# First-norm modulation on TensorE for both samples, and a first FFN block fed tile by tile

## The chip, the core and the metric

One core of one Trainium2 chip runs the kernel. A core has TensorE (PE: matmul; PEld is its weight load), VectorE (DVE), ScalarE (ACT), GpSimd (POOL) and SyncE (SP), which here issues every DMA. The metric is the device time of one execution in microseconds, the median of several runs. All data is fp32; large products are made from rounded parts ("high" and "low"), three matmuls for each pair of tiles.

## What is computed

One layer of a diffusion backbone, for 1024 latent tokens and 256 context tokens of width 1024. Cut to what matters here:

```python
m = silu(cvec) @ w_mod + b_mod                # nine vectors of 1024, for c (latent) and for c_ctx (context)
def pre(h, g_pre, shift, scale):
    return rms_norm(h, g_pre) * (1.0 + scale) + shift
ffn1 = lambda h, m: 0.5 * post(swiglu(pre(h, norm_pre[0], m[0], m[1]), w_gate, w_up, w_down), norm_post[0], m[2])
x, h_c = x + ffn1(x, mx), h_c + ffn1(h_c, mc)   # mx from c, mc from c_ctx
# then the token mixers (attention and a gated recurrence), and a second FFN for x alone
```

Vector 0 (shift) and vector 1 (scale) of either sample have to be known before the first FFN can read its input.

## The kernel before

Activations lie transposed: width on the 128 partitions in KT = 8 slices, tokens along the free axis, in three chunks `CH`: 0 and 1 of 512 latent tokens (sample 0), 2 of 256 context tokens (sample 1). The first FFN walks the 2816 hidden columns in 11 blocks of two 128-column tiles `f`. Block 0 runs `block_by_chunk`: for a chunk `gu` makes the gate and up products (4 PSUM tiles named bank; with `k_outer` the contraction index k runs outermost, so that k = 0 can start when one input slice is there), then `down` multiplies with two rows of the down weights into PSUM tiles y. Later blocks run `block`, over all chunks. `heads` says which chunks share one pass of block 0: chunks 0 and 1 first, then chunk 2 in a pass of its own, which loads the block's weights again.

`load_w` loads 512 KB to a staging tile st (three buffers), casts the high part on ScalarE (line 91) and subtracts on VectorE or GpSimd for the low part (line 92). In block 0 GpSimd does that for three of the four gate and up tiles.

`start1(i)` prepares chunk i: `row_norms` (squares, column sums on TensorE at line 217, the reciprocal root by `rsqrt` in eleven small VectorE steps, a diagonal, and at line 233 a matmul with ones that spreads it over the partitions; cb is the PSUM of both), then `build_u` with four operations for each slice: GpSimd multiplies by the row, ScalarE applies scale and shift (line 459) and casts `uh` (line 460), GpSimd subtracts for `ul` (line 461). Before each slice, `mod_first` loads two 512 KB tiles of w_mod (one output per partition) and VectorE makes a dot product of each with the conditioning row `crow[s]` (line 153); it does so for sample 0 before chunk 0 and again for sample 1 while chunk 1 is built. The other seven vectors come later as tasks (`mod_stream`) spread over the middle blocks.

Each engine runs its instructions in a fixed order that a scheduler made when the kernel was built; `tc.high_priority()` moves some forward. DMAs are issued in SP's order, and one that waits for its buffer holds all behind it.

Of the kernel before, what the change touches and what calls it, by code (L numbers as in the profile page):

```python
# [14 lines left out]
ALU = mybir.AluOpType  # L15
# [32 lines left out]
def f32(ap):  # L48
    return ap.bitcast(F32)
# [3 lines left out]
def hybrid_block(ctx: ExitStack, tc: tile.TileContext, xT, cc, cols, w_mod, w_gate, w_up, w_down, w_tok, w_col,  # L53
# [101 lines left out]
    def mod_first(d, s, st, split=False):  # L155
        for m in (1, 0):
            t = st()
            sp.dma_start(out=t, in_=w_mod[m * KT + d])
            to = mods[:, m, d, s:s + 1]
            if split and m == 0:  # L160
                pool.tensor_tensor(t, t, crow[s], op=ALU.mult)
                act.activation(t, t, AF.Copy, accum_out=to)
            else:
                dot(t, t, crow[s], to)
            finish_mod(m, slice(d, d + 1), slice(s, s + 1))

    def mod_stream(ms, junkp):
        halves = []

        def step(m, d):  # L170
            ss = range(2 if m < 5 else 1)
            st = stp.tile([P, D], F32, name="st")
            sp.dma_start(out=st, in_=w_mod[m * KT + d])
# [12 lines left out]
        return [(lambda m=m, d=d: step(m, d)) for m in ms for d in range(KT)]  # L186
# [118 lines left out]
    def ffn(which, chunks, heads, ends, ys, wp, hp, psA, psB, finish, start, pump, tasks=(), before=lambda sub: None):  # L305
# [10 lines left out]
        def gu(ws, sub, k_outer=False, pump=None):  # L316
# [7 lines left out]
            for j, e, k in order:  # L324
                w = ws[j][e]
# [97 lines left out]
    with f1_ctx:  # L423
# [27 lines left out]
        def build_u(i, before):  # L451
            o, n = CH[i]
            s = 1 if i == 2 else 0
            for d in range(KT):
                before(d)
                u32 = nrm.tile("xt", n) if i in (2,) else sl(n)
                h = uh[i][:, d, :]
# [5 lines left out]
        spare = ys[2].rearrange("p a b -> p (a b)").rearrange("p (t d) -> p t d", d=D)  # L463
        turn = [0]

        def stage():
            return stp.tile([P, D], F32, name="st")

        def next_spare():
            turn[0] += 1  # L470
            return spare[:, turn[0] % 2] if turn[0] % 3 else stage()

        def start1(i):
            if i == 0:
                with tc.high_priority():
                    row_norms(0)

                def before(d):
                    mod_first(d, 0, next_spare)
                    if d == 4:  # L480
                        fetch(1)
                    if d == 7:
                        row_norms(1)

                build_u(0, before)
                fetch(2)
                sp.dma_start(out=crow[1], in_=cc[1:2].partition_broadcast(P))
                act.activation(crow[1], crow[1], AF.Silu)
            elif i == 1:
                def before(d):  # L490
                    if d == 4:
                        row_norms(2)
                    mod_first(d, 1, stage)

                build_u(1, before)
            else:
                build_u(2, lambda d: None)

        sp.dma_start(out=crow[0], in_=cc[0:1].partition_broadcast(P))
        sp.dma_start(out=col, in_=cols)  # L500
        act.activation(crow[0], crow[0], AF.Silu)
        fetch(0)
        def finish1(sub):
# [3 lines left out]
        ffn(0, FULL, ((1, FULL[0:2]), (1, FULL[2:3])),  # L507
            ((((2, 0, 256), (0, 0, 512)),) * 2, (((1, 0, 512),), ((1, 0, 256), (1, 256, 256)))),
            ys, w1, hp, psA, psB, finish1, start1, nrm.pump, tasks)
# [658 lines left out]
def layout(a):  # L1168
# [5 lines left out]
    def cols(w, n=P):  # L1174
# [6 lines left out]
        "cc": np.concatenate([a["c"], a["c_ctx"][None]]),  # L1181
        "cols": lines(a["b_mod"], a["norm_pre"], a["norm_post"], a["hg_norm"], a["hg_lower_bound"]),
        "w_mod": a["w_mod"][0].T.reshape(9 * KT, P, D),
# [31 lines left out]
```

## Time and profile before

| | us |
|---|---|
| median of 3 runs | 2861.35 (2856.90 to 2863.21) |
| the profiled execution | 2862.51 |
| its span, first to last instruction | 2860.7 |
| TensorE busy | 2730.9 (95%) |
| VectorE busy | 1542.4 (54%) |
| ScalarE busy | 1009.6 (35%) |
| GpSimd busy | 352.8 (12%) |

TensorE's share is near the whole span, so what an edit is worth depends on where TensorE waits. Busy TensorE is not TensorE at its peak: a matmul can be held by its weight load or run at the lower of two granted clock levels (0.50 or 1.00 in the column PEclk; before the first recorded change, at 40.9 us, the column reads 1.00 whatever the level was). In the order lists and in the trace one fp32 matmul of the norm stands as two records.

### The profile page before, as it was taken

Reading aid. Unit: us, or ns where it says so; the run is one execution under the profiler, and the core shown is the slowest. Engines: PE = TensorE matmul, PEld = TensorE weight load, DVE = VectorE, ACT = ScalarE, POOL = GpSimd, SP = SyncE. Lnnn points to the kernel's source line nnn. Section 1 sums busy time; section 2 is a strip of 40 time slices with the busy share of each in tenths; the row PEclk is TensorE's granted clock in tenths of the full one; section 3 lists DMA queues with packets and bytes.
Section 4 is the critical chain, followed back from the end, with each engine's and each line's share of the span. In section 5 each row is a group of like instructions: output and inputs, shape, how many; then the busy total and the mean of one; then the engine's idle time right before and its main releaser. Section 6 shows DMA issues by size and latency. Waiting matters only on the chain.

```text
span 2860.7 us, 37319 instructions
## 1 busy us (share of the span) xinstructions
PE 2730.9 (95%) x15032; PEld 2332.9 (82%) x15032; DVE 1542.4 (54%) x2893; ACT 1009.6 (35%) x1495; POOL 352.8 (12%) x276
## 2 busy tenths in 40 slices
PE   4799999999999988999999988899989999999998
PEld 3588888888888888889988877787878888888887
DVE  7756554444435785656655488644474333333336
ACT  3521111111112442566776565343354211111123
POOL 4600000000000332100000132212141000000002
PEclk9899999999999999999999999999999999999999
DMA  6552222322212432211111233254353211111123
GB/s 228 175 161 93 77 75 81 96 85 85 67 45 64 136 108 71 74 50 50 38 57 44 79 136 124 78 183 141 111 170 107 74 52 52 45 45 46 58 67 103
DMA packets 114702, 259.48 MB, mean 91 GB/s; under 512 B 12256, under 2 KB 51808, under 8 KB 114528
## 3 DMA queue, kind: packets, MB, share of 16 engines
q1 hardware_dynamic: 114528, 257.08, 28.4%
q8 instruction: 118, 1.93, 0.3%
q14 instruction: 56, 0.46, 0.0%
HBM read 216.67 MB, written 40.37 MB: 90 GB/s over the span
## 4 chain that ended last, share of the span: by engine, by line
PE 71%; DVE 10%; issue 8%; ACT 4%; DMA 4%; POOL 2%; SPq 0%; DVEq 0%; POOLq 0%; ACTq 0%
PE bank L101 12%; PE bank L102 12%; PE bank L100 12%; PE y L100 6%; PE y L101 6%; PE y L102 6%; PE fb L101 2%; PE fb L102 2%; PE fb L100 2%; PE S L749 2%; PE bank L765 1%; DMA gt<-gate_d 1%; PE po L778 1%; DVE w L92 1%; PE po L779 1%
## 5 line engine op out<-in xcount | busy, mean ns | idle before, releaser
L100 PE MATMUL bank<-uh,w 128*128 128x512 f32 (+1 forms) x1952 | 715.2, 368 | 15.0 <-ACT uh L460 12.5
L101 PE MATMUL bank<-ul,w 128*128 128x512 f32 (+1 forms) x1952 | 717.7, 368 | 7.0 <-POOL ul L461 6.9
L102 PE MATMUL bank<-uh,w 128*128 128x512 f32 (+1 forms) x1952 | 716.2, 367 | 1.8 <-DVE w L92 1.8
L91 ACT CAST w<-st 128x1024 fp32r<-128x1024 f32 x234 | 243.3, 1049 | 785.9 <-PE y L101 439.8
L100 PEld LDWEIGHTS bank<-uh,w 128*128 128x128 f32 x1952 | 370.8, 190 | 75.5 <-ACT uh L460 14.4
L101 PEld LDWEIGHTS bank<-ul,w 128*128 128x128 f32 x1952 | 371.5, 190 | 68.8 <-POOL ul L461 10.1
L102 PEld LDWEIGHTS bank<-uh,w 128*128 128x128 f32 x1952 | 372.1, 191 | 60.7 <-DVE w L92 2.7
L92 DVE TENSOR_TENSOR w<-st,w 128x1024 fp32r<-128x1024 f32 x212 | 267.2, 1268 | 255.1 <-ACT w L91 253.1
L355 DVE TENSOR_TENSOR y<-y,y 128x512 f32<-128x512 f32 (+1 forms) x416 | 255.0, 619 | 202.7 <-PE y L102 200.8
L100 PE MATMUL y<-h,w 128*128 128x512 f32 (+1 forms) x736 | 283.4, 387 | 8.9 <-ACT h L341 3.9
L102 PE MATMUL y<-h,w 128*128 128x512 f32 (+1 forms) x736 | 281.1, 383 | 1.4 <-DVE w L92 1.4
L101 PE MATMUL y<-h,w 128*128 128x512 f32 (+1 forms) x736 | 281.7, 383 | 0.3 <-DVE h L342 0.3
L340 DVE TENSOR_TENSOR sl<-bank,sl 128x512 f32<-128x512 f32 (+1 forms) x114 | 70.5, 620 | 373.4 <-PE bank L102 365.7
L268 POOL TENSOR_TENSOR y<-y,xt 128x512 f32<-128x512 f32 x48 | 64.0, 1352 | 1551.7 <-DVE y L267 891.4
L100 PE MATMUL fb<-uh,w 128*128 128x512 f32 (+1 forms) x576 | 222.6, 387 | 0.0
L102 PE MATMUL fb<-uh,w 128*128 128x512 f32 (+1 forms) x576 | 220.1, 382 | 0.0
L101 PE MATMUL fb<-ul,w 128*128 128x512 f32 (+1 forms) x576 | 220.0, 382 | 0.0
L100 PEld LDWEIGHTS y<-h,w 128*128 128x128 f32 x736 | 138.4, 189 | 42.2 <-ACT h L341 5.7
L102 PEld LDWEIGHTS y<-h,w 128*128 128x128 f32 x736 | 139.0, 189 | 28.9 <-DVE w L92 2.0
L101 PEld LDWEIGHTS y<-h,w 128*128 128x128 f32 x736 | 139.1, 189 | 25.4 <-DVE h L342 0.8
L341 ACT CAST h<-sl 128x512 fp32r<-128x512 f32 (+1 forms) x92 | 55.3, 602 | 281.0 <-DVE sl L340 280.7
L339 ACT ACTIVATE sl<-bank 128x512 f32<-128x512 f32 (+1 forms) x114 | 61.0, 537 | 189.5 <-PE bank L102 189.5
(225 smaller groups left out, 4307.2 us busy)
## 6 DMA issues: line engine op xcount, KB each, us to landing
st<-in_w_mod SPq DMA_DIRECT2D x77, 512.0 KB, 3.7
st<-in_w_gate SPq DMA_DIRECT2D x56, 512.0 KB, 3.7
st<-in_w_up SPq DMA_DIRECT2D x56, 512.0 KB, 3.7
st<-in_w_down SPq DMA_DIRECT2D x56, 512.0 KB, 3.6
st<-in_w_col SPq DMA_DIRECT2D x32, 512.0 KB, 3.7
gate_d<-ft SPq DMA_DIRECT2D x32, 256.0 KB, 2.4
gt<-gate_d SPq DMA_DIRECT2D x32, 256.0 KB, 2.8
st<-in_w_o SPq DMA_DIRECT2D x16, 512.0 KB, 3.7
```

Of the source, the lines that this page charges most:

```text
L91: act.copy(hi, st)
L92: eng.tensor_tensor(lo, st, f32(hi), op=ALU.subtract)
L100: pe.matmul(ps, lh, rh, start=first, stop=False)
L101: pe.matmul(ps, lh, rl, start=False, stop=False)
L102: pe.matmul(ps, ll, rh, start=False, stop=last)
L268: pool.tensor_tensor(yj, yj, xt, op=ALU.add)
L339: act.activation(sl, pg, AF.Silu)
L340: dve.tensor_tensor(sl, pu, sl, op=ALU.mult)
L341: act.copy(hh, sl)
L355: dve.tensor_tensor(yd, py, yd, op=ALU.add)
L749: pe.matmul(S[:, cs_], qT[:, (s * 2 + t) * P:(s * 2 + t + 1) * P], kT[g][:, cs_], start=(s == 0), stop=(s == 1))
L765: pe.transpose(pt[:, (a * 2 + t) * P:(a * 2 + t + 1) * P], prob[t][:, kt * P:(kt + 1) * P], ident)
```

## The change

- Vectors 0 and 1 are made by TensorE for both samples at once: a 512 KB tile of w_mod01 now has the contraction on its partitions; eight matmuls of 128x128 weights against two columns (`cs_t`, both conditioning vectors) give a [128, 2] result (line 164 of the changed kernel), and one small VectorE operation finishes it. There are 16 such tiles, where sample 0 and sample 1 had 16 loads each. Four spare buffers take turns.
- Slices are fed inside the product: `feed(i, k)` is called at each k of chunk 0's first product, makes the vectors two slices ahead and builds the slice one ahead.
- `build_u` has three operations: VectorE multiplies by scale and row, ScalarE adds the shift and casts `uh`, VectorE makes `ul`. GpSimd has no part in block 0 any more; all four weight subtractions are VectorE's.
- The loads of chunks 1 and 2 follow all vector tiles; `row_norms(1)` and `row_norms(2)` move behind the products of the chunk ahead.
- `heads` is one pass of block 0 over all three chunks; four gate and up tiles and two down rows are loaded once less.

```diff
-    def mod_first(d, s, st, split=False):
+    def mod_first(d, st, bank):
         for m in (1, 0):
             t = st()
-            sp.dma_start(out=t, in_=w_mod[m * KT + d])
-            to = mods[:, m, d, s:s + 1]
...
-                dot(t, t, crow[s], to)
-            finish_mod(m, slice(d, d + 1), slice(s, s + 1))
+            sp.dma_start(out=t, in_=w_mod01[m * KT + d])
+            ps = bank()[:, 0:2]
+            for k in range(KT):
+                pe.matmul(ps, t[:, k * P:(k + 1) * P], cs_t[:, k, :], start=(k == 0), stop=(k == KT - 1))
+            if m == 1:
+                dve.tensor_scalar(gpre[:, 0, d, :], ps, bias1[:, d:d + 1], npre[:, 0, d:d + 1],
+                                  op0=ALU.add, op1=ALU.mult)
+            else:
+                dve.tensor_scalar(mods[:, 0, d, :], ps, bias_c[:, 0, d:d + 1], None, op0=ALU.add)
...
             for j, e, k in order:
+                if k_outer and j == 0 and e == 0:
+                    feed(i, k)
...
-            eng = pool if b == 0 and which == 0 else dve
-            gw = [(gcol(w_gate, f, eng), gcol(w_up, f, eng if f == fs[0] else dve)) for f in fs]
+            gw = [(gcol(w_gate, f), gcol(w_up, f)) for f in fs]
...
-                pool.tensor_tensor(u32, ys[i][:, d, :], rows[i], op=ALU.mult)
-                act.activation(u32, u32, AF.Identity, bias=mods[:, 0, d, s:s + 1], scale=gpre[:, 0, d, s:s + 1])
-                act.copy(h, u32)
-                pool.tensor_tensor(ul[i][:, d, :], u32, f32(h), op=ALU.subtract)
+            dve.scalar_tensor_tensor(u32, ys[i][:, d, :], gpre[:, 0, d, s:s + 1], rows[i], op0=ALU.mult, op1=ALU.mult)
+            act.activation(h, u32, AF.Identity, bias=shift)
+            dve.scalar_tensor_tensor(ul[i][:, d, :], u32, shift, f32(h), op0=ALU.add, op1=ALU.subtract)
...
+        def feed1(i, k):
+            if i:
+                return
+            if k == 0:
+                build_u(0, 0)
+            if k + 2 < KT:
+                mod_first(k + 2, next_spare, nrm.bank)
+            elif k == KT - 2:
+                fetch(1)
+                fetch(2)
+                for s in range(2):
+                    sp.dma_start(out=crow[s], in_=cc[s:s + 1].partition_broadcast(P))
+            if k + 1 < KT:
+                build_u(0, k + 1)
...
-        ffn(0, FULL, ((1, FULL[0:2]), (1, FULL[2:3])),
+        ffn(0, FULL, ((1, FULL),),
```

What TensorE has in a row at its start, before:

```order
L217 MATMUL cb<-ones,acc 128x1 x4
L233 MATMUL cb<-sq,ones 128x128 x4
L100 MATMUL bank<-uh_90,w 128x512
L101 MATMUL bank<-ul_93,w 128x512
L102 MATMUL bank<-uh_90,w 128x512
```

And after (lines 221 and 237 are the 217 and 233 of before):

```order
L221 MATMUL cb<-ones,acc 128x1 x4
L237 MATMUL cb<-sq,ones 128x128 x4
L164 MATMUL cb<-cs_t,crow_135 128x2 x8
L164 MATMUL cb<-cs_t,y_125 128x2 x8
L164 MATMUL cb<-cs_t,crow_136 128x2 x8
L100 MATMUL bank<-uh_90,w 128x512 x3
L164 MATMUL cb<-cs_t,y_125 128x2 x8
L100 MATMUL bank<-uh_90,w 128x512
L101 MATMUL bank<-ul_93,w 128x512
L102 MATMUL bank<-uh_90,w 128x512
```

Three vector tiles now stand ahead of chunk 0's first product; the others follow one by one, with six or seven of its 96 matmuls between two of them, and 16 behind the last.

TensorE where chunk 0's products end and chunk 1's begin (uh_90 is chunk 0's input, uh_91 chunk 1's), before:

```order
L100 MATMUL y<-h,w 128x512
L101 MATMUL y<-h,w 128x512
L100 MATMUL y<-h,w 128x512
L101 MATMUL y<-h,w 128x512
L102 MATMUL y<-h,w 128x512 x2
L100 MATMUL bank<-uh_91,w 128x512 x3
```

And after:

```order
L102 MATMUL bank<-uh_90,w 128x512
L221 MATMUL cb<-ones,acc 128x1 x4
L237 MATMUL cb<-sq,ones 128x128 x4
L100 MATMUL y<-h,w 128x512
L101 MATMUL y<-h,w 128x512
L100 MATMUL y<-h,w 128x512
L101 MATMUL y<-h,w 128x512
L100 MATMUL bank<-uh_91,w 128x512 x2
L102 MATMUL y<-h,w 128x512 x2
```

The two steps of chunk 1's norm, which stood inside chunk 0's products, now stand between the two chunks.

ScalarE around the same place, after (line 450 squares chunk 1 or 2, 346 and 348 are the gated unit of chunk 0, 455 copies the spread row):

```order
L464 ACTIVATE uh_90<-sl,mods 128x512 x8
L450 ACTIVATE acc<-y_117 128x512
L450 ACTIVATE sq<-y_117 128x512
L346 ACTIVATE sl<-bank 128x512
L450 ACTIVATE sq<-y_117 128x512
L346 ACTIVATE sl<-bank 128x512
L348 CAST h<-sl 128x512
L450 ACTIVATE sq<-y_117 128x512 x2
L348 CAST h<-sl 128x512
L450 ACTIVATE sq<-y_117 128x512 x3
```

Before, the eight squares of chunk 1 stood among the casts of chunk 0's slices; now six of them come after the first gated unit.

## Rows read from the trace of the kernel before

**Rows 1.** The page's busy time of each engine.

```profile
PE 2730.9 (95%) x15032; PEld 2332.9 (82%) x15032; DVE 1542.4 (54%) x2893; ACT 1009.6 (35%) x1495; POOL 352.8 (12%) x276
```

**Rows 2.** Busy us (instructions) by engine, granted clock, DMA; stretches of 40 us.

```profile
core 0: us, PE busy (x) PEld busy (x) DVE busy (x) ACT busy (x) POOL busy (x), PEclk, DMA share, GB/s
0.00:40.00 40.00, 9.80 (x28) 7.32 (x28) 26.32 (x49) 15.79 (x21) 15.78 (x14) 1.00 0.66 227
40.00:80.00 40.00, 29.04 (x101) 21.48 (x102) 32.07 (x61) 16.85 (x29) 19.56 (x13) 0.83 0.68 234
...
200.00:240.00 40.00, 40.00 (x210) 34.19 (x209) 20.88 (x45) 5.12 (x8) 0.00 (x0) 1.00 0.25 79
```

**Rows 3.** TensorE timeline: start us, us, line, out<-in, count [idle before <-releaser].

```profile
170.20 0.28 PE L102 MATMUL y<-hc,w 128*128 128x256 f32 x1
```

**Rows 4.** TensorE timeline: the records of chunk 0's norm.

```profile
14.64 1.87 PE L217 MATMUL cb<-ones,acc 128*128 128x1 f32 x8 [14.64 <-DVE acc L446]
23.40 2.08 PE L233 MATMUL cb<-sq,ones 128*128 128x128 f32 x8 [6.89 <-DVE sq L227]
```

**Rows 5.** TensorE timeline, chunk 0: wide matmuls and their spacing.

```profile
44.36 0.79 PE L101 MATMUL bank<-ul,w 128*128 128x512 f32 x1 [2.90 <-POOL ul L461]
...
46.66 0.63 PE L102 MATMUL bank<-uh,w 128*128 128x512 f32 x1
47.09 0.63 PE L100 MATMUL bank<-uh,w 128*128 128x512 f32 x1
...
47.87 0.40 PE L102 MATMUL bank<-uh,w 128*128 128x512 f32 x1
...
77.12 0.39 PE L101 MATMUL bank<-ul,w 128*128 128x512 f32 x1
77.35 0.39 PE L102 MATMUL bank<-uh,w 128*128 128x512 f32 x1
```

**Rows 6.** TensorE timeline at 952 us: column sums among wide matmuls.

```profile
952.31 0.95 PE L217 MATMUL cb<-ones,acc 128*128 128x1 f32 x8
953.11 0.48 PE L100 MATMUL bank<-uh,w 128*128 128x512 f32 x1
```

**Rows 7.** Busy us by engine and granted clock, as rows 2, four short stretches.

```profile
157.10:160.30 3.20, 1.77 (x14) 1.55 (x13) 1.82 (x4) 2.77 (x5) 0.00 (x0) 1.00 0.00 0
160.50:163.70 3.20, 2.75 (x16) 2.27 (x16) 3.20 (x5) 1.23 (x2) 0.00 (x0) 1.00 0.78 200
928.50:931.70 3.20, 2.23 (x14) 2.01 (x15) 3.10 (x8) 0.80 (x2) 0.00 (x0) 1.00 0.98 267
931.90:935.10 3.20, 3.20 (x9) 2.52 (x8) 1.19 (x3) 0.00 (x0) 0.00 (x0) 0.50 1.03 408
```

**Rows 8.** TensorE timeline within the third of those stretches.

```profile
930.04 0.95 PE L217 MATMUL cb<-ones,acc 128*128 128x1 f32 x8
```

**Rows 9.** VectorE timeline, chunk 0's norm and weights.

```profile
9.92 4.67 DVE L446 TENSOR_TENSOR acc<-acc,sq 128x512 f32<-128x512 f32 x6
...
17.10 2.25 DVE L196 SCALAR_TENSOR_TENSOR nw<-rc 128x4 f32<-128x4 f32 x1
...
21.88 0.16 DVE L196 SCALAR_TENSOR_TENSOR nw<-rc 128x4 f32<-128x4 f32 x1
...
27.08 1.44 DVE L92 TENSOR_TENSOR w<-st,w 128x1024 fp32r<-128x1024 f32 x1 [1.61 <-ACT w L91]
```

**Rows 10.** ScalarE timeline: copy of a spread row, cast of a weight.

```profile
25.51 0.58 ACT L449 COPY acc<-cb 128x512 f32<-128x512 f32 x1 [8.69 <-PE cb L233]
...
78.67 1.05 ACT L91 CAST w<-st 128x1024 fp32r<-128x1024 f32 x1 [0.40 <-DMA st<-in_w_down]
```

**Rows 11.** TensorE timeline: the spreads of chunks 1 and 2.

```profile
73.05 1.05 PE L233 MATMUL cb<-sq,ones 128*128 128x128 f32 x8
...
106.91 1.19 PE L233 MATMUL cb<-sq,ones 128*128 128x128 f32 x4 [8.71 <-DVE sq L227]
```

**Rows 12.** The page's DMA issues: queue, count, KB each, median us to landing.

```profile
st<-in_w_mod SPq DMA_DIRECT2D x77, 512.0 KB, 3.7
```

More of the change, by code (lines that the diff above doesn't have):

```diff
@@ L52, in hybrid_block @@
 @with_exitstack
-def hybrid_block(ctx: ExitStack, tc: tile.TileContext, xT, cc, cols, w_mod, w_gate, w_up, w_down, w_tok, w_col,
+def hybrid_block(ctx: ExitStack, tc: tile.TileContext, xT, cc, cT, cols, w_mod01, w_mod, w_gate, w_up, w_down, w_tok, w_col,
                  w_mrg, w_o, q_norm, k_norm, cos_t, sin_t, mask_f, mask_b, out_t, out_e):
@@ L153, in dot @@
         dve.scalar_tensor_tensor(junk, st, 1.0, row, op0=ALU.mult, op1=ALU.mult, accum_out=out)
[L155 removed]
+    cs_t = const.tile([P, KT, 2], F32, name="cs_t")
+    bias1 = const.tile([P, KT], F32, name="bias1")
+    def mod_first(d, st, bank):
         for m in (1, 0):
             t = st()
[L158 to L165 removed]
+            sp.dma_start(out=t, in_=w_mod01[m * KT + d])
[5 more added lines that the diff above has]
+                                  op0=ALU.add, op1=ALU.mult)
+            else:
+                dve.tensor_scalar(mods[:, 0, d, :], ps, bias_c[:, 0, d:d + 1], None, op0=ALU.add)
     def mod_stream(ms, junkp):
@@ L172, in step @@
             st = stp.tile([P, D], F32, name="st")
-            sp.dma_start(out=st, in_=w_mod[m * KT + d])
+            sp.dma_start(out=st, in_=w_mod[(m - 2) * KT + d])
             if d == 0:
@@ L303, in drain, with ffn @@
                 self.pump()
-    def ffn(which, chunks, heads, ends, ys, wp, hp, psA, psB, finish, start, pump, tasks=(), before=lambda sub: None):
+    def ffn(which, chunks, heads, ends, ys, wp, hp, psA, psB, finish, start, pump, tasks=(), before=lambda sub: None,
+            feed=lambda i, k: None):
         tasks = list(tasks)
@@ L449, in row_norms, with build_u @@
             act.copy(rows[i], ps)
-        def build_u(i, before):
-            o, n = CH[i]
+        def build_u(i, d):
+            n = CH[i][1]
             s = 1 if i == 2 else 0
[L454 to L457, printed above, removed]
-                pool.tensor_tensor(u32, ys[i][:, d, :], rows[i], op=ALU.mult)
-                act.activation(u32, u32, AF.Identity, bias=mods[:, 0, d, s:s + 1], scale=gpre[:, 0, d, s:s + 1])
-                act.copy(h, u32)
-                pool.tensor_tensor(ul[i][:, d, :], u32, f32(h), op=ALU.subtract)
+            u32 = nrm.tile("xt", n) if i == 2 else sl(n)
+            h = uh[i][:, d, :]
+            shift = mods[:, 0, d, s:s + 1]
+            dve.scalar_tensor_tensor(u32, ys[i][:, d, :], gpre[:, 0, d, s:s + 1], rows[i], op0=ALU.mult, op1=ALU.mult)
+            act.activation(h, u32, AF.Identity, bias=shift)
+            dve.scalar_tensor_tensor(ul[i][:, d, :], u32, shift, f32(h), op0=ALU.add, op1=ALU.subtract)
         spare = ys[2].rearrange("p a b -> p (a b)").rearrange("p (t d) -> p t d", d=D)
+        spares = [spare[:, 0], crow[0], spare[:, 1], crow[1]]
         turn = [0]
-        def stage():
-            return stp.tile([P, D], F32, name="st")
         def next_spare():
             turn[0] += 1
-            return spare[:, turn[0] % 2] if turn[0] % 3 else stage()
+            return spares[turn[0] % 4]
         def start1(i):
@@ L476, in start1 @@
                     row_norms(0)
[L478 to L485, printed above, removed]
-                fetch(2)
[L487 to L495, printed above, removed]
-            else:
-                build_u(2, lambda d: None)
-        sp.dma_start(out=crow[0], in_=cc[0:1].partition_broadcast(P))
+                for d in range(2):
+                    mod_first(d, next_spare, nrm.bank)
+            elif i == 1:
+                row_norms(1)
+                for d in range(KT):
+                    build_u(1, d)
+            else:
+                row_norms(2)
+                for d in range(KT):
+                    build_u(2, d)
+        def feed1(i, k):
[7 more added lines that the diff above has]
+                fetch(1)
+                fetch(2)
+                for s in range(2):
+                    sp.dma_start(out=crow[s], in_=cc[s:s + 1].partition_broadcast(P))
+            if k + 1 < KT:
+                build_u(0, k + 1)
+            else:
+                for s in range(2):
+                    act.activation(crow[s], crow[s], AF.Silu)
+        sp.dma_start(out=cs_t, in_=cT)
         sp.dma_start(out=col, in_=cols)
-        act.activation(crow[0], crow[0], AF.Silu)
+        act.activation(cs_t, cs_t, AF.Silu)
+        dve.tensor_scalar(bias1, bias_c[:, 1], 1.0, None, op0=ALU.add)
         fetch(0)
@@ L1181, in layout @@
         "cc": np.concatenate([a["c"], a["c_ctx"][None]]),
+        "cT": np.concatenate([a["c"], a["c_ctx"][None]]).reshape(2, KT, P).transpose(2, 1, 0),
         "cols": lines(a["b_mod"], a["norm_pre"], a["norm_post"], a["hg_norm"], a["hg_lower_bound"]),
-        "w_mod": a["w_mod"][0].T.reshape(9 * KT, P, D),
+        "w_mod01": cols(a["w_mod"][0][:, 0:2 * D]).reshape(2 * KT, P, D),
+        "w_mod": a["w_mod"][0][:, 2 * D:].T.reshape(7 * KT, P, D),
         "w_gate": np.stack([cols(w).reshape(NF, P, D) for w in a["ffn_w_gate"][0]]),
```

2 lines of the change are left out of this document (1 added, 1 removed).

## The prediction, made before the changed kernel was run

> **What bounds the kernel now.** I read the page first: TensorE is busy 2730.9 us, 95% of the 2860.7 us span [rows 1]. So the kernel as a whole is a TensorE kernel, and a saving on VectorE, ScalarE or the DMA queue counts only where TensorE waits for it. The table of 40 us stretches says where that is [rows 2]: TensorE is busy 9.8 of the first 40 us, 29 of the next, and all of the forty from 200 us on. The change touches only what happens before that point, so I read that part as a timeline of each engine and asked one thing: when is block 0 of the first FFN done? Its last matmul ends at 170.5 us; 13 matmuls of block 1 (3 us) already stand ahead of it, so block 0 costs 167.5 us [rows 3]. Two marks cut this in stages:
>
> - Start to 25.5 us: squares of chunk 0, the column sums (eight one-column records, 14.64), the reciprocal root on VectorE, the spread (23.40) [rows 4].
> - 25.5 to 77.7 us: the 96 wide (512-column) matmuls of chunk 0. Back to back they would need 22 us at the upper clock level, where they stand some 0.2275 us apart (0.23 by 77.12 and 77.35), and 41 us at the lower, 0.427 apart (46.66, 47.09) [rows 5]. The rest is waiting for the input tiles, which wait for the dot products of VectorE.
> - 77.7 to 167.5 us: everything else of block 0, 89.8 us.
>
> **The change part by part.** *Added on TensorE: the 16 vector tiles.* Each is eight fp32 matmuls of two columns with weights of their own, so 16 records, as the column sums give two records for each matmul. The trace has no two-column ones; the nearest rows are the one-column and the 128-column ones, and they cost the same: at the lower level eight take 1.87 us and 2.08 us with the tail of the last, some 0.21 us each [rows 4]; at the upper level eight of one column push the next wide matmul from 952.31 to 953.11, 0.10 us each [rows 6]. So a tile costs 16 x 0.21 = 3.4 us or 16 x 0.10 = 1.6 us, and the sixteen 54 or 26 us. None of it lies beside other work of TensorE: it runs in order, and the new order puts three tiles ahead of the first wide matmul and one after each six or seven of them. A gain below zero is excluded, since no TensorE work is taken away in exchange.
>
> *Which level?* In the trace the stretch from 928.5 to 931.7 has TensorE busy 2.23 us, 0.95 of them column sums (930.04), and the granted clock is 0.50 right behind it; from 157.1 to 160.3 it is busy less, 1.77 us, but all of it 512- and 256-column work, and the clock stays at 1.00 [rows 7, 8]. The small matmuls did not hold the upper level. It also rises late: at 47.8 only after eight wide matmuls had stood without a gap from 44.36 on [rows 5]. In the changed order at most seven stand between two vector tiles. So I take the lower level (1.2 GHz) from the start of the stage until the last tile; behind it 16 wide ones stand together. The upper level is the other bound.
>
> The Trainium skill (TensorE: Matmul & The Clock Gate, Why this matters for your kernels) advises to keep TensorE continuously busy to get the full clock. Read literally, this dense stream of tiny matmuls would be at 2.4 GHz; no run here shows it, and it is the first rival below.
>
> *The start* does not move. VectorE takes over three weight subtractions from GpSimd (1.44 us each, 27.08), set between the steps of the root, some 4 us; but there one step of 128x4 (17.10) had taken 2.25 us and the next as much beside GpSimd's subtractions, against 0.16 for the same step at 21.88 [rows 9]. That 4 us goes. I keep 25.5.
>
> *End of chunk 0's products*, at the lower level: 25.5 + 54 + 96 x 0.427 (41) = 120.5, less 1 us for the last 16, in which the level may rise: 119.5 us, against 77.7. The build of the input hides: per step of the contraction VectorE has two 512-element operations (0.8 us each by six in 4.67) and ScalarE one (0.58) [rows 9, 10], against 12 us of TensorE. The loads hide too: 512 KB land in 3.7 us [rows 12], and a vector tile's buffer is taken again after four tiles, over 20 us of TensorE.
>
> *Moved: the norm of chunk 1.* Today its spread (73.05) and the column sums before it stand inside the products of chunk 0 [rows 11]. In the changed program both stand between the products of chunk 0 and those of chunk 1, and ScalarE has the sigmoid-weighted units of chunk 0 mixed with the last six squares. Behind the end of the products: two more steps of the gated unit and five or six squares of 0.6 us, some 4.6 us (0.58 for 512 elements, 25.51) [rows 10]; from the last addition (14.59) to the spread row's copy (26.1) chunk 0's chain took 11.5 us [rows 9, 10], 4.2 of them beside GpSimd's subtractions, so 7.3; then one weight cast (1.05, 78.67) and a start of 0.3. TensorE waits 13.3 us. On SP the loads of chunk 1, chunk 2, the two conditioning rows and the first down weights now queue behind the vector tiles, and chunk 2's last half waits for the last tile's matmuls, 6.5 us before the products end; the 3 MB in front of and with the down weights take 13 us at 234 GB/s [rows 2], which lands 8 us behind the end and is covered by those 13.3.
>
> *Chunk 1's products:* 100 matmuls x 0.2275 = 22.8, and 2.5 for restarting at the lower level. *Norm of chunk 2,* after them in the new order: 6.5 us (the same chain, two columns fewer, squares done). *Chunk 2's products,* half as wide: 96 x 0.12 = 11.5, and 2.5 again. *Down products:* 90 x 0.2275 + 48 x 0.12 = 26.2, with 4.5 for the second down weight, whose buffers only come free now, and for evacuation. Sum: 13.3 + 25.3 + 6.5 + 14 + 30.7 = 89.8 us, the same as today's 89.8.
>
> *Removed:* the sixteen loads and dots for sample 1, GpSimd's whole part, and the second loading of four block-0 weights and two down weights. They held TensorE up in the third stage (8.7 us before 106.91 for chunk 2's spread alone [rows 11]); those savings are already in the 89.8, and the norm waits take their place. From block 1 on both programs do the same work.
>
> **Sum.** 119.5 + 89.8 = 209.3 us against 167.5: 41.8 us later. The profiled execution took 2862.5 us for a span of 2860.7, 1 us above the median of 2861.35, so the sum goes on the median: 2903 us. Its bounds: a norm wait of 10 to 17 us and tiles of 3.2 to 3.6 us give 2896 to 2910.
>
> **Rivals.** *1. The tiny matmuls keep the clock up.* All tiles but the first two at the upper level: 25.5 + 26 + 22 + 4 = 77.5 us, then the same 89.8: 167.3 against 167.5, no change, 2861; with the bounds of the norm wait 2857 to 2867. For it: the stage would be dense. Against it: [rows 7, 8].
>
> *2. The level rises and falls within the stage.* Seven wide matmuls in a row nearly repeat what preceded the rise at 47.8. If a third to two thirds of the 95 us run at the upper level, 16 to 32 us come back: 2871 to 2887; edges 2867 to 2895.
>
> *3. Faster: the weight loads hide.* The decider is whether the tiles' 256 weight loads run beside the wide matmuls. Then only the first three tiles cost their 3.4 us; with the wide ones at the upper level the stage ends at 25.5 + 10 + 22 + 4 = 61.5, 16 us earlier: 2845. It decides from less than 1.6 us per tile on. Against it: in the steady part loads for wide matmuls already hold the weight port 34.2 of 40 us [rows 2], and column sums placed among wide matmuls pushed them by the full 0.10 each [rows 6].
>
> By a rule of the Trainium skill (TensorE: Matmul & The Clock Gate, Part 2, step by step) weight loads are pulled ahead of running matmuls; that is this rival's mechanism, and [rows 6] show it hiding nothing where small matmuls follow each other.
>
> **How the numbers follow.** Lower level throughout: 0.50. Rival 2: 0.23. Rival 1: 0.17. Rival 3: 0.10. About 0.2% (5.7 us) is what a measurement of this kernel can tell from no change. Slower by more: 0.50 + 0.23 + 0.03 of rival 1's upper edge = 0.76; same 0.14; faster 0.10. The range runs from 2863, inside rival 1, to 2912, 2 us above the first case's own bound: it leaves out rival 3, half of rival 1 and little above, 2 in 10.
>
> **What would show it.** Right: the vector tiles' 16 records take about 3.4 us each, wide matmuls between them 0.43 apart, granted clock 0.5 until near 115 us, chunk 0's last product near 119 us, then a TensorE gap of some 13 us before chunk 1, block 0 done near 209 us, and the same pace after. Wrong: records of 0.10 us and 0.23 us spacing before 60 us (rival 1), alternating levels (rival 2), tiles that do not delay the wide matmuls (rival 3); or a gap before chunk 1 far from 13 us, which would fault my reading of the moved norm.

## The result, and the profile after

| | before | after |
|---|---|---|
| median | 2860.8 us | 2903.7 us (4 runs, 2894.04 to 2905.37) |
| ratio | | 1.014, 95% interval 1.0126 to 1.0154 |
| profiled execution | 2862.51 us | 2904.91 us |

The change makes the kernel 1.4% slower. The predicted 2903 us is met by luck: in the traces below block 0 is done 26 us earlier than forecast, and the rest of the kernel takes 26 us longer.

The page's busy time of each engine, after (before: [rows 1]):

```profile
PE 2793.9 (96%) x15288; PEld 2379.1 (82%) x15288; DVE 1496.5 (52%) x2846; ACT 991.4 (34%) x1466; POOL 269.3 (9%) x222
```

TensorE has 256 records more (the vector tiles) and 63 us more busy time; VectorE and GpSimd have less to do. The first two stretches of [rows 2], after:

```profile
0.00:40.00 40.00, 21.97 (x93) 20.92 (x93) 16.16 (x37) 12.47 (x17) 0.70 (x6) 1.00 0.62 212
40.00:80.00 40.00, 40.00 (x197) 36.16 (x198) 8.45 (x18) 2.90 (x4) 0.00 (x0) 1.00 0.38 114
```

TensorE no longer waits from 40 to 80 us (40.0 busy, before 29.0): the starved stage became a dense one. What the dense stage consists of stands in the TensorE timeline, after (start us, us, line, out<-in, count [idle before <-releaser]):

```profile
12.42 1.87 PE L221 MATMUL cb<-ones,acc 128*128 128x1 f32 x8 [12.42 <-DVE acc L452]
19.90 2.08 PE L237 MATMUL cb<-sq,ones 128*128 128x128 f32 x8 [5.61 <-DVE sq L231]
21.77 3.41 PE L164 MATMUL cb<-cs_t,crow 128*128 128x2 f32 x16
25.04 3.55 PE L164 MATMUL cb<-cs_t,y 128*128 128x2 f32 x16
28.45 3.55 PE L164 MATMUL cb<-cs_t,crow 128*128 128x2 f32 x16
...
43.96 0.63 PE L100 MATMUL bank<-uh,w 128*128 128x512 f32 x1
44.39 0.63 PE L101 MATMUL bank<-ul,w 128*128 128x512 f32 x1
...
64.44 2.06 PE L164 MATMUL cb<-cs_t,crow 128*128 128x2 f32 x16
...
67.84 1.84 PE L164 MATMUL cb<-cs_t,y 128*128 128x2 f32 x16
69.54 0.49 PE L100 MATMUL bank<-uh,w 128*128 128x512 f32 x1
...
93.30 0.39 PE L102 MATMUL bank<-uh,w 128*128 128x512 f32 x1
99.84 1.86 PE L221 MATMUL cb<-ones,acc 128*128 128x1 f32 x8 [6.15 <-DVE acc L452]
104.25 2.08 PE L237 MATMUL cb<-sq,ones 128*128 128x128 f32 x8 [2.55 <-DVE sq L231]
108.25 0.80 PE L100 MATMUL y<-h,w 128*128 128x512 f32 x1 [1.93 <-ACT w L91]
...
133.56 0.50 PE L221 MATMUL cb<-ones,acc 128*128 128x1 f32 x4
...
140.92 1.01 PE L100 MATMUL bank<-uh,w 128*128 128x256 f32 x3 [1.52 <-ACT uh L464]
...
183.56 0.28 PE L102 MATMUL y<-hc,w 128*128 128x256 f32 x1
```

Read from the top: three vector tiles follow each other without a gap for 10 us at 3.4 us each, with wide matmuls 0.43 apart behind them (43.96, 44.39): the lower level, 1.2 GHz, although TensorE was dense. The trace records the rise to 2.4 GHz at 64.9 us, inside the tile at 64.44; from there a tile costs 1.7 us (67.84 to the next wide matmul at 69.54). Chunk 0's products end at 93.7 us, then come 14.5 us with only the norm of chunk 1, and block 0's last matmul ends at 183.8; two matmuls of block 1 stand ahead of it, so block 0 is done at 183.4 us, 15.9 later than before. The other 26 us come later. I matched the TensorE records of the two traces by tile, counted from the end, and took the difference of their starts:

| us of the kernel before | lag of after |
|---|---|
| 200 to 900 (rest of the first FFN) | 15.8, falling to 15.2 |
| 1110 | 20.3 |
| 1900 | 18.1 |
| 2010, start of the second FFN | 20.2 |
| 2160 | 24.2 |
| 2800 | 42.0 |

In the second FFN nothing was changed. From 2150 us (before) and 2170 us (after) to its end both profiles have it at the upper level and with less than 1 us of TensorE waits; yet it does less in the same time. One stretch of 100 us, before and after (columns as in [rows 2]):

```profile
2300.00:2400.00 100.00, 100.00 (x443) 82.71 (x442) 37.23 (x48) 15.59 (x20) 0.00 (x0) 1.00 0.14 43
```

```profile
2300.00:2400.00 100.00, 100.00 (x430) 80.48 (x429) 34.45 (x45) 15.25 (x20) 0.00 (x0) 1.00 0.16 48
```

443 matmuls are 226 ns each, 430 are 233: wide matmuls start 226 to 227 ns apart before and 230 to 238 after, with the same engines at work beside them.

### The profile page after: what moved, and what is told of

It reads as the page before. It is cut to its first block, busy times and chain, and to the rows that moved or that the text cites. A ratio compares the mean times of both kernels' runs of the same rounds, so it can differ in the third digit from the quotient of the medians.

```text
span 2902.8 us, 37652 instructions
## 1 busy us (share of the span) xinstructions
PE 2793.9 (96%) x15288; PEld 2379.1 (82%) x15288; DVE 1496.5 (52%) x2846; ACT 991.4 (34%) x1466; POOL 269.3 (9%) x222
## 5 line engine op out<-in xcount | busy, mean ns | idle before, releaser
L91 ACT CAST w<-st 128x1024 fp32r<-128x1024 f32 x228 | 237.0, 1049 | 799.4 <-PE y L101 445.7
```

The costliest lines, as they stand in the source:

```text
L91: act.copy(hi, st)
```

## Theories

*A (placement).* The new constants cs_t and bias1 take 96 bytes per partition, and all that is allocated behind them on that side of SBUF (uh, ul, the hidden tiles h) moves up by 96. The weights of the second FFN lie at the other end and stay. In the built program uh0 starts at byte 5504 before and 5600 after, the first of those weights at 180096 in both; slices of uh are 2048 bytes apart, those of a weight 512, so that the distance of moving tile and weight modulo 512 is the same for all matmuls there: 0 before, 416 after. *Rival:* something that the new program leaves behind (its order, its DMA queue, 256 more records).

*B (level).* The vector tiles do not raise the clock level; the stage is long while it is low. *Rival:* the time of the rise does not depend on TensorE's work. *C (moved norm)*: the 14.5 us are the price of the norm's new place. *D:* of the parts of the change, GpSimd's removal helps and the vectors on TensorE cost.

All experiments, each with the kernel before timed on the same chip (2861.3 to 2862.6 us). "Block 0" is worked out as above, from the profiled run.

| kernel | median us | ratio, 95% interval | block 0 done |
|---|---|---|---|
| before | 2860.8 | 1 | 167.5 |
| after | 2903.7 | 1.0126 to 1.0154 | 183.4 |
| a_pad32 | 2892.1 | 1.0088 to 1.0118 | 180.1 |
| a_w2pad | 2895.8 | 1.0093 to 1.0129 | 171.8 |
| a_same | 2874.6 | 1.0027 to 1.0053 | 177.3 |
| b_pad96 | 2880.6 | 1.0047 to 1.0080 | 167.8 |
| b_pad128 | 2880.5 | 1.0045 to 1.0075 | 168.2 |
| a_warm | 2868.2 | 1.0014 to 1.0041 | 176.6 |
| a_norm | 2874.6 | 1.0029 to 1.0059 | 173.7 |
| b_nogp | 2840.9 | 0.9905 to 0.9935 | 146.5 |
| b_nogp1 | 2845.6 | 0.9925 to 0.9954 | 150.2 |
| b_late | 2844.7 | 0.9920 to 0.9950 | 149.1 |
| b_best | 2848.3 | 0.9943 to 0.9972 | 151.1 |
| b_final | 2834.8 | 0.9894 to 0.9927 | 138.6 |

## Experiments on the second FFN

**a_pad32**, the changed kernel:

```diff
     bias1 = const.tile([P, KT], F32, name="bias1")
+    const.tile([P, 8], F32, name="pad")
```

> The changed kernel with one unused tile of 32 bytes per partition behind bias1. The two new constant tiles (cs_t, bias1) take 96 bytes per partition, so every tile allocated behind them on that side of SBUF, among them uh, ul and the hidden tiles h, starts 96 bytes later than in the kernel before; the weights of the second FFN lie on the other side and do not move. With the 32 bytes the shift is 128. Theory (placement: moving tile and weight in different 32-byte halves of a 64-byte line cost some 3 to 10 ns per wide matmul): the lag behind the kernel before stays near the 16 us it has at 200 us, the spacing of wide matmuls in the second FFN returns from 230-238 ns to 227, time 2877 to 2883. Rival (the lag after block 0 comes from something that block 0 leaves behind: the order, the DMA queue, the clock): 2900 to 2905, spacing 230-238 as before.

**b_pad96**, the kernel before:

```diff
     gpost = const.tile([P, 3, KT, 2], F32, name="gpost")
+    const.tile([P, 24], F32, name="pad")
```

> The kernel before with one unused constant tile of 96 bytes per partition and no other edit: the placement of the changed kernel without the change. Theory (placement): no difference in block 0 (167 us), then slower, at least 17 us of it in the second FFN, 2878 to 2888. Rival (placement is not it): 2856 to 2863.

The same stretch of b_pad96:

```profile
2300.00:2400.00 100.00, 100.00 (x430) 80.48 (x429) 37.68 (x51) 14.04 (x18) 0.00 (x0) 1.00 0.15 48
```

An unused tile of 96 bytes costs 18 us, and gives the same 430 matmuls as the changed kernel: theory A holds for the kernel before. But a_pad32 came out at 2892 and lost 18 us in the second FFN all the same:

```profile
2300.00:2400.00 100.00, 100.00 (x432) 80.85 (x431) 38.03 (x51) 14.66 (x19) 0.00 (x0) 1.00 0.14 43
```

It missed both expected ranges, and my form of the theory, halves of 64 bytes, falls.

**a_w2pad**, the changed kernel:

```diff
     edge.tile([P, 24], F32, name="edge")
+    edge.tile([P, 8], F32, name="pad")
     wp = w2_ctx.enter_context(tc.tile_pool(name="ffn2w", bufs=12, side="right", reuse_waits="tile"))
```

> The changed kernel with 32 unused bytes ahead of the weights of the second FFN, so that these too start at 32 modulo 64, like uh, ul and h there; nothing else moves. If what counts is that weight and moving tile start in the same half of a 64-byte line: the second FFN loses its drift of 17 us, 2883 to 2889. If what counts is that tiles start on a 64-byte line: no gain or a further loss, 2900 to 2915. If placement is not it: 2900 to 2905.

```profile
2300.00:2400.00 100.00, 100.00 (x432) 81.08 (x431) 40.28 (x52) 15.63 (x20) 0.00 (x0) 1.00 0.16 47
```

No gain: 18 us lost again in the second FFN, and 2896 lies in none of the three ranges. This kernel and a_pad32 both have the distance 384 modulo 512 (180096 less 5632, 180064 less 5600), and both have 432 matmuls. So I took the distance modulo a larger power of two as the cause.

**a_same**, the changed kernel, with nothing at another address than before:

```diff
-    cs_t = const.tile([P, KT, 2], F32, name="cs_t")
-    bias1 = const.tile([P, KT], F32, name="bias1")
+    cs_t = mods[:, 1]
+    bias1 = mods[:, 8, :, 1]
```

> The changed kernel with cs_t and bias1 laid into columns of mods that nothing else uses, so that no tile of the program stands at another address than in the kernel before; the instructions are the same. Theory (what the second FFN loses is a matter of where uh, ul, h and w stand to each other, with a period of 512 bytes: before, uh and w of the second FFN stand 512 x 341 bytes apart, in the changed kernel 96 bytes off that, with the 32-byte tile 128 off, in every one of these the second FFN lost 17 to 21 us): wide matmuls of the second FFN 227 ns apart again, the lag stays what block 0 leaves (4 to 16 us), 2865 to 2879. Rival (the new program itself, its 256 more TensorE records or its DMA order, slows the second FFN; the alignment to 64 bytes alone was refuted by the 32-byte tile): 2888 to 2900.

**b_pad128**, the kernel before:

```diff
+    const.tile([P, 32], F32, name="pad")
```

> The kernel before with one unused constant tile of 128 bytes per partition, no other edit: the offset between uh and w of the second FFN that the changed kernel with the 32-byte tile has. Theory (period above 128 bytes): block 0 unchanged, the second FFN 16 to 20 us longer, 2877 to 2885. Rival (128 bytes is a whole period, and what the 32-byte tile left was another cause): 2858 to 2866.

The stretch in a_same, then in b_pad128:

```profile
2300.00:2400.00 100.00, 100.00 (x443) 82.56 (x442) 40.29 (x52) 16.02 (x20) 0.00 (x0) 1.00 0.15 44
```

```profile
2300.00:2400.00 100.00, 100.00 (x432) 80.85 (x431) 36.73 (x48) 14.05 (x18) 0.00 (x0) 1.00 0.14 46
```

Both as theory A says: a_same has 443 again and its lag stays at 14.6 to 14.9 from 2160 us to the end; b_pad128 has the 432 of the other two kernels with that distance. Seven kernels give three distances, and each distance has its own number: 443 at 0, 430 at 416, 432 at 384. The program's order, its DMA and its record count do not matter for this spacing. The change by itself costs 0.4% (a_same). Of the other 1.0%, 29 us, the place of its two constants is shown to cost some 18 (b_pad96, b_pad128). In the profiled runs of the changed kernel and a_same, 27 us apart, 20 lie in the second FFN (a lag that grows from 20.2 to 42.0, against 13.3 to 14.9) and 6 in block 0 (183.4 against 177.3), whose length varies from run to run, as the next section shows. Distances other than these three were not tried, nor what in the memory makes them differ.

## Experiments on block 0

Four kernels above have the changed kernel's order in block 0, and give a second result for nothing. The level rose at 64.9 us in the first trace, at 58.4 in a_pad32, 52.2 in a_same and 39.4 in a_w2pad, and chunk 0's last product began at 93.30, 90.25, 87.24 and 81.31. The later the rise, the longer the stage, by half the difference, as two levels of factor two must have it; from chunk 0's end on, block 0 took 89.5 to 90.1 us in all four. Each of the four rises came within half a us of the end of a group of six or seven wide matmuls; in three of the four, groups as long had passed before without one. The rows of a_same, then of a_w2pad (columns as above):

```profile
39.62 3.41 PE L164 MATMUL cb<-mods,crow 128*128 128x2 f32 x16
...
51.99 1.95 PE L164 MATMUL cb<-mods,crow 128*128 128x2 f32 x16
...
87.24 0.39 PE L102 MATMUL bank<-uh,w 128*128 128x512 f32 x1
```

```profile
39.61 1.84 PE L164 MATMUL cb<-cs_t,crow 128*128 128x2 f32 x16
...
81.31 0.39 PE L102 MATMUL bank<-uh,w 128*128 128x512 f32 x1
```

The same instructions take 3.41 us a tile in one run and 1.84 in the other at the same place. So the stage has no one length. This would also explain why the changed kernel's runs spread over 11 us and a_same's over 12, where those of the kernel before spread over 3 to 8; but only one run of each has a trace.

**a_warm**, on a_same:

```diff
+            if warm is not None:
+                for _ in range(8):
+                    pe.matmul(full, warm[:, 0:P], warm[:, 0:512], start=True, stop=True)
...
+            if d < 2:
+                for _ in range(6):
+                    pe.matmul(full, ident_r, ident_r.unsqueeze(1).broadcast_to([P, 4, P]), start=True, stop=True)
```

> As a_same (changed kernel, placement of before), with unused 512-column matmuls added on TensorE: 8 of the third weight tile between chunk 0's column sums and its spread, where TensorE idled 5.6 us, and 6 ahead of each of the first four vector tiles; the scheduler also sets two squares of chunk 1 earlier. Their results are overwritten and read by nobody. In four runs of the unchanged order the granted clock rose at 39.4, 52.2, 58.4 and 64.9 us and chunk 0's last product began at 81.3, 87.2, 90.3 and 93.3: the later the rise, the longer the stage, by half the difference. Theory (the vector tiles cannot raise the level, but hold it once wide matmuls have raised it): rise before 30 us, vector tiles 1.7 us each, chunk 0's last product at 75 to 79 us for all the 24 extra matmuls, 2859 to 2867, and less spread between runs. Rival 1 (the tiles pull the level down again, since so few wide ones stand among the first): alternating levels, stage no shorter, 2873 to 2884. Rival 2 (the time of the rise is not set by what TensorE does): rise anywhere from 39 to 65 us, 18 to 24 extra matmuls at 0.43 us come on top, 2878 to 2888.

TensorE timeline of a_warm:

```profile
14.66 2.93 PE L246 MATMUL cb<-w 128*128 128x512 f32 x6 [0.39 <-ACT w L94]
...
21.64 1.84 PE L171 MATMUL cb<-mods,crow 128*128 128x2 f32 x16
...
31.70 1.84 PE L171 MATMUL cb<-mods,y 128*128 128x2 f32 x16
33.40 1.93 PE L171 MATMUL cb<-mods,crow 128*128 128x2 f32 x16
35.97 2.35 PE L171 MATMUL cb<-mods,y 128*128 128x2 f32 x16
...
42.17 3.41 PE L171 MATMUL cb<-mods,crow 128*128 128x2 f32 x16
```

The level rose at 20.1 us, 5.4 us after the first unused wide matmul, so the rise does follow TensorE's work, against rival 2; but it fell again at 37.1, after two tiles directly behind each other (31.70, 33.40) and a third only three wide matmuls later, and alternated until 81.5: rival 1. The 32 unused matmuls are paid for with a few us to spare (2868.2 against 2874.6, intervals that overlap); the time lies between the ranges of the theory and of rival 1.

**a_norm**, on a_same:

```diff
             elif i == 1:
-                row_norms(1)
                 for d in range(KT):
                     build_u(1, d)
+                row_norms(2)
             else:
-                row_norms(2)
                 for d in range(KT):
...
+            if k == 1:
+                fetch(1)
+            if k == 5:
+                row_norms(1)
             if k + 2 < KT:
                 mod_first(k + 2, next_spare, nrm.bank)
             elif k == KT - 2:
-                fetch(1)
                 fetch(2)
```

> As a_same, with the norms moved back into the products: chunk 1 is loaded behind the sixth vector tile and its squares, column sums and spread stand inside chunk 0's products; chunk 2's norm inside chunk 1's. Theory (the moved norms cost the changed kernel a TensorE gap of 14.5 us before chunk 1, part of it at the lower level it leads to, and some 5 us before chunk 2): the gap before chunk 1 shrinks to 2 to 4 us, 12 to 16 us in all, 2858 to 2864. Rival (the norm's chain on VectorE and ScalarE, or the earlier loads, then delay chunk 0's slices and vector tiles; or TensorE waits as long for the next thing, the down weights): 2868 to 2876.

TensorE timeline of a_norm:

```profile
49.62 1.84 PE L164 MATMUL cb<-mods,crow 128*128 128x2 f32 x16
51.32 1.93 PE L164 MATMUL cb<-mods,y 128*128 128x2 f32 x16
54.99 1.22 PE L100 MATMUL bank<-uh,w 128*128 128x512 f32 x2 [1.74 <-ACT uh L464]
56.01 3.41 PE L164 MATMUL cb<-mods,crow 128*128 128x2 f32 x16
...
106.59 0.79 PE L100 MATMUL y<-h,w 128*128 128x512 f32 x1 [3.11 <-ACT w L91]
```

The gap before chunk 1 shrank from 14.5 to 3.1 us as expected, and the time did not move (2874.6 in both, in the rival's range). The scheduler's new order sets two vector tiles directly behind each other (49.62, 51.32); as in a_warm the level, up since 40.5, fell right after them, at 54.2, and chunk 0's last product began at 103.09 instead of 87.24, with 56 us of the stage at the lower level against 30 in a_same. TensorE also waited 1.7 us for a slice there (54.99), so that a_norm by itself does not show which of the two brought the level down; in a_warm there was no such wait. In the four kernels above six or seven wide matmuls stand between any two tiles behind the rise, and the level held to the end of the stage. The gap was real, but in its place came a longer stage.

**b_nogp**, the kernel before:

```diff
-            eng = pool if b == 0 and which == 0 else dve
+            eng = dve
...
-                pool.tensor_tensor(u32, ys[i][:, d, :], rows[i], op=ALU.mult)
-                act.activation(u32, u32, AF.Identity, bias=mods[:, 0, d, s:s + 1], scale=gpre[:, 0, d, s:s + 1])
-                act.copy(h, u32)
-                pool.tensor_tensor(ul[i][:, d, :], u32, f32(h), op=ALU.subtract)
+                shift = mods[:, 0, d, s:s + 1]
+                dve.scalar_tensor_tensor(u32, ys[i][:, d, :], gpre[:, 0, d, s:s + 1], rows[i], op0=ALU.mult, op1=ALU.mult)
+                act.activation(h, u32, AF.Identity, bias=shift)
+                dve.scalar_tensor_tensor(ul[i][:, d, :], u32, shift, f32(h), op0=ALU.add, op1=ALU.subtract)
```

> One part of the change alone, on the kernel before: GpSimd is taken out of block 0 (build_u with three operations, the product with the row and the low part on VectorE; all four weight subtractions on VectorE), while the vectors stay dot products on VectorE and block 0 keeps its two passes. Placement is that of the kernel before. Theory 1 (the 3.5 us that the start gained in the changed kernel come from VectorE being free of GpSimd's subtractions beside it): the first spread moves from 23.4 to about 20, block 0 gets 3 to 10 us shorter, 2851 to 2858. Rival (VectorE, which makes the dot products, is what chunk 0 waits for, and two more operations per slice lengthen the stage): block 0 some 5 to 10 us longer, 2866 to 2871.

More than twice as good as theory 1 had it: 21 us. Two of VectorE's groups in block 0 (line, operation, shapes, count | busy us, mean ns of one | idle before), before and in b_nogp:

```profile
L153 DVE SCALAR_TENSOR_TENSOR y<-y,crow 128x1024 f32<-128x1024 f32 x11 | 16.6, 1511 | 0.0
L145 DVE TENSOR_TENSOR mods<-mods,col 128x1 f32<-128x1 f32 x32 | 13.0, 409 | 0.5
```

```profile
L153 DVE SCALAR_TENSOR_TENSOR y<-y,crow 128x1024 f32<-128x1024 f32 x11 | 13.3, 1218 | 1.8 <-DMA y<-in_w_mod 1.8
L145 DVE TENSOR_TENSOR mods<-mods,col 128x1 f32<-128x1 f32 x32 | 4.5, 151 | 0.0
```

Both became faster: a one-column addition 151 ns instead of 409, a dot product 1218 instead of 1511. In the trace of the kernel before, the 17 of the 32 additions that overlap a GpSimd operation take 633 ns on average, the 15 others at most 160: waiting for GpSimd had been booked as busy time. VectorE took over 54 operations of 0.5 to 1.2 us (6 weight subtractions, 48 for the slices), and its busy time in the first 200 us even fell, from 147.6 to 144.3 us. The Trainium skill (SBUF — State Buffer, Who interferes with whom) has it that VectorE and GpSimd share a pair of ports under an exclusive lock, and that a VectorE instruction with two inputs in SBUF contends with a GpSimd one that reads SBUF; these rows agree. The start, on which theory 1 rested, did not gain: the first spread stands at 23.59 us, as before (23.40).

**b_nogp1**, on b_nogp:

```diff
-        ffn(0, FULL, ((1, FULL[0:2]), (1, FULL[2:3])),
+        ffn(0, FULL, ((1, FULL),),
```

> The kernel before without GpSimd in block 0 (as b_nogp, 2841) and with block 0 in one pass over the three chunks: two parts of the change without the vectors on TensorE and without the feeding. Six weight tiles are loaded, cast and subtracted once less (6 x 1.2 us of VectorE, which is busy 19 of each 20 us there). Theory (VectorE bounds block 0): 4 to 8 us less than b_nogp, 2833 to 2838. Rival (the pass order brings chunk 2's norm and build in front of the down products that covered them): 2841 to 2850.

The rival holds: one pass costs about 4 us instead of saving them (3.7 in block 0, 4.7 in the medians). The pool has ten weight buffers and one pass needs twelve, so the second down weight, and with it nearly all down products, waits for chunk 2.

**b_late**, on b_nogp1:

```diff
-                def before(d):
-                    if d == 4:
-                        row_norms(2)
-                    mod_first(d, 1, stage)
-
-                build_u(1, before)
+                build_u(1, lambda d: None)
+                row_norms(2)
             else:
-                build_u(2, lambda d: None)
+                build_u(2, lambda d: mod_first(d, 1, stage))
```

> As b_nogp1, with the dot products of sample 1 moved from the build of chunk 1 to that of chunk 2, which is the first to need them, and chunk 2's norm ahead of them. Theory: chunk 1's build no longer waits for 16 dot products (1.2 us each), which then lie beside chunk 1's products: block 0 done near 125 to 135 us, 2822 to 2832. Rival (TensorE then stands before chunk 2's products, with the down products queued behind them): 2835 to 2845.

**b_best**: the same move on b_nogp (two passes), and `fetch(0)` ahead of the load of crow[0].

> As b_nogp (2841: the kernel before, without GpSimd in block 0), two passes again, with the dot products of sample 1 moved to the build of chunk 2 and the first load of chunk 0 issued ahead of the conditioning row. In b_late the same move of the dot products left TensorE 7 us ahead of b_nogp at 100 us, and lost that before chunk 2, because the down products stood behind it: with one pass the second down weight has no free buffer until chunk 2's products are done. With two passes the down products stand ahead of chunk 2. Theory: the 7 us stay, 2 us more at the start: 2828 to 2834. Rival (VectorE's sum of work sets the end of block 0, whatever its order): 2837 to 2843.

Both theories missed: 2844.7, in the rival's range, and 2848.3, above either range. In b_late the 7 us won by 100 us went in front of chunk 2, with the down products queued behind it (TensorE busy 9.9 of the next 20 us). In b_best these stood ahead of it, and TensorE starved all the same. The queue's timeline shows why, with a part of the stretch in which it waited (columns as in [rows 2]):

```profile
61.24 0.33 SPq L88 DMA_DIRECT2D st<-in_w_up  x1
90.65 0.33 SPq L88 DMA_DIRECT2D st<-in_w_gate  x1
...
95.19 34.50 SPq L158 DMA_DIRECT2D st<-in_w_mod  x16
```

```profile
80.00:100.00 20.00, 19.35 (x85) 15.09 (x85) 10.07 (x22) 9.82 (x16) 0.00 (x0) 1.00 0.33 96
```

Sixteen loads stood behind the second pass's weights, whose buffers were in use until 90 us, while VectorE, which makes the dot products, was busy 10.1 of 20 us and the DMA moved 96 GB/s.

**b_final**, on b_best:

```diff
                 row_norms(2)
+                for d in range(KT):
+                    mod_first(d, 1, stage)
             else:
-                build_u(2, lambda d: mod_first(d, 1, stage))
+                build_u(2, lambda d: None)
```

> As b_best, with sample 1's dot products moved once more, to the end of chunk 1's build, so that their sixteen loads stand in SP's queue ahead of the second pass's weights. In b_best TensorE had lost 46 us by 100 us (b_nogp 58, the kernel before 68) and then lost 22 more: the loads waited from 61 to 95 us behind weights whose buffers were still in use, while VectorE idled 6.8 us and the DMA queues moved 65 GB/s. Theory (that queue was the cause): the dot products run from 78 us on, chunk 2's input is ready when the down products end, loss by 160 us about 50 us, 2828 to 2835. Rival (VectorE's sum of work sets the end in any order): 2838 to 2843, as b_nogp.

The queue's timeline of b_final, and the stretch behind it:

```profile
57.25 50.27 SPq L158 DMA_DIRECT2D st<-in_w_mod  x16
```

```profile
80.00:100.00 20.00, 19.55 (x89) 15.44 (x88) 17.40 (x51) 7.61 (x14) 0.00 (x0) 1.00 0.74 214
```

The loads begin at 57 us, VectorE is busy 17.4 of the same 20 us (from 60 to 80 us the DMA moves little in both, 65 and 69 GB/s), block 0 is done at 138.6 instead of 151.1, and the kernel takes 2834.8 us (2831.7 to 2841.9): faster than the kernel before by 0.7 to 1.1%, and than the changed one by 2.4%. Its interval overlaps that of b_nogp (0.9905 to 0.9935), which has the larger part of the gain.

## Why the prediction was right, point by point

- **Number, sign:** 2903 against 2903.7, but by errors that cancel: the number is luck. Of the prediction's own signs the price of a tile, the spacing of 0.43 before the rise and the gap before chunk 1 came; the lower level until 115 us, the last product near 119, block 0 near 209 and the same pace after it did not. Without the placement the same change takes 2874.6 (a_same), which lies in rival 2's 2871 to 2887.
- **Price of a tile:** right at both levels, 3.4 us (21.77, 25.04) and 1.7 (1.6 predicted). None of it was hidden (rival 3 falls), and the tiles alone did not raise the level (rival 1 falls): dense for 10 us, at 1.2 GHz. The Trainium skill's advice to keep TensorE busy (TensorE: Matmul & The Clock Gate, Why this matters for your kernels), read literally, does not hold for these rows.
- **"So I take the lower level from the start of the stage until the last tile":** the first step that failed. The level rose at 64.9 us and held to the end of the stage; 29 us ran at 2.4 GHz. It rested on one rise, at 47.8 us behind eight wide matmuls [rows 5], against at most seven here. The same trace has another, at 61.4, behind seven wide ones and the column sums:

```profile
58.06 0.79 PE L101 MATMUL bank<-ul,w 128*128 128x512 f32 x1 [0.39 <-POOL ul L461]
...
61.21 1.05 PE L217 MATMUL cb<-ones,acc 128*128 128x1 f32 x8
```

  The runs show no fixed place at all, 39 to 65 us in four traces. The rise made the stage 22 us shorter than predicted (115.8, with the start as measured, against 93.7).
- **"The start does not move":** it moved by 3.7 us. Column sums began at 12.42 instead of 14.64 [rows 4]: the conditioning row's 512 KB load no longer stands ahead of chunk 0 (in b_best, where it stands behind, they began at 11.32). The wait for the root was 1.3 us shorter (5.61 against 6.89): the term that was mis-sized is the three weight subtractions. The two slow steps beside GpSimd did go (2.25 us each, 0.16 without [rows 9]), but a subtraction between two steps of the root, as here in the timeline of VectorE after, holds the root up by 1.02 us and not by 1.44, three of them by 3.1 us:

```profile
14.81 1.23 DVE L92 TENSOR_TENSOR w<-st,w 128x1024 fp32r<-128x1024 f32 x1
15.95 0.15 DVE L201 TENSOR_TENSOR nw<-nw 128x4 f32<-128x4 f32 x1
```

  In b_nogp a dot product stands there as a fourth operation, and the wait is 6.62; in b_best there is one, and it is 3.57:

```profile
21.91 1.22 DVE L153 SCALAR_TENSOR_TENSOR y<-y,crow 128x1024 f32<-128x1024 f32 x1
```

- **The moved norm:** a gap of 13.3 predicted, 14.5 measured, of the kind named (squares, root, spread, weight cast). In a_norm, the one order tried with the norms moved back, the time did not fall.
- **The rest of block 0:** 89.8 us predicted from chunk 0's end, 89.7 measured, and by its terms, in their order: 14.5, 25.3, 7.4, 14.3 and 28.2 against 13.3, 25.3, 6.5, 14 and 30.7. The second down weight did not hold TensorE up.
- **"From block 1 on both programs do the same work":** the second step that failed, by 26 us. The work is the same; its place in SBUF is not. 22 of these us arise in the second FFN, 21 in b_pad96, with the same placement. About 5 arise from 900 to 1110 us, and these go with the clock: over the same work the granted clock is 0.94 on average in after, a_same and a_w2pad, which lose 4.5 to 5 us there, and 0.96 before and in a_pad32, which loses none. 2 are regained by 1900 and lost again by 2010.
- **GpSimd's removal:** counted only at the start and in "held TensorE up in the third stage". It is the one part that was seen to gain: 21 us alone (b_nogp). All parts together end 12.5 us above the kernel before (a_same), so the vectors on TensorE, with the feeding and the one pass that come with them, cost some 34 us (21.3 + 12.5) if the parts add up; the one pass is 4 to 5 of them (b_nogp1).

## What to carry to other kernels

A change that allocates something, however small, can move everything behind it; compare the spacing of untouched matmuls in both traces before explaining a difference, and test a new tile's effect with an unused tile of its size in the old kernel. As in this stage, small matmuls that fill TensorE's idle time can cost the clock level of the wide ones beside them, and a stage near that edge has a length that varies from run to run. Ahead of any new arithmetic, take GpSimd off the time in which VectorE is the bound, and look at what stands in the DMA queue ahead of the loads that the bound waits for.

## What the runs showed of the hardware

- Wide matmuls start 226 to 227 ns apart where moving tile and weight lie a multiple of 512 bytes apart in the partition (443 in 100 us), and 228 to 241 ns at distances of 384 (432) and 416 (430) modulo 512, at full granted clock, with the same load beside it: 18 us of this kernel. Other distances were not tried.
- Three groups of sixteen records of two-column fp32 matmuls kept TensorE dense for 10 us (21.77 to 31.87) without a rise of the level; behind eleven unused wide matmuls it rose 5.4 us after the first (14.66 to 20.1).
- A VectorE addition of one column, both inputs in SBUF, took 633 ns on average where it overlapped a GpSimd operation, and at most 160 where it did not; in b_nogp, without GpSimd, 151.
